# One hybrid diffusion trunk on one core: RG-LRU gate products in 64x64 quarters of TensorE, the scan result rounded on VectorE, the first norm kept off GpSimd, modulation weights loaded in halves

## The chip, the cores and the metric

The kernel runs on one core of one Trainium2 chip. The time is device microseconds of one execution. Five engines run side by side, each in the order of its own instruction list: TensorE (PE for its products, PEld for its weight loads), VectorE (DVE), ScalarE (ACT), GpSimd (POOL) and SyncE (SP), which here issues all transfers.

## The reference

Two layers of a trunk over 256 context and 256 latent tokens of width 1024. Each layer: a modulated RMS norm, an input projection, three token mixers (RG-LRU, gated linear attention, grouped attention), a gated merge, an output projection, then a modulated norm and an MLP. The change touches the modulation, the first norm and the RG-LRU:

```python
h = modulate(x, norm1_g, sh1, sc1)          # rms_norm(x, g) * (1 + scale) + shift
xh = xc.reshape(bn, n, LRU_BLOCKS, LRU_BLOCK_W)          # 16 blocks of 64 channels
r = sigmoid(einsum('bnhi,hij->bnhj', xh, a_w) + a_b)
i = sigmoid(einsum('bnhi,hij->bnhj', xh, x_w) + x_b)
log_a = -RGLRU_C * r * softplus(-lam)
u = sqrt(-expm1(2.0 * log_a)) * (i * xc)
# h_t = exp(log_a_t) * h_(t-1) + u_t, forward and backward; y = (h_0 + h_1) * gelu(y_in)
```

The inputs are float32. The gates exist for two directions, so each 128-channel tile of `xc` has four products with block-diagonal weights: two 64x64 blocks each.

## The kernel before

Activations are held with channels on the 128 partitions, in 8 tiles of width 1024/8, and with all 512 tokens along the row (in the last layer mixers whose context output nobody reads use the last 256 tokens only, `c0 = 256`). A float32 product of width 1024 is made of float32r products: operands are split into a rounded part and a rest (`hh`/`hl`, `wh`/`wl`), and `gemm` (L256) issues three matmuls of 512 columns for each of 8 channel tiles. A weight tile is loaded by SP (`weight_raw`, L189, three buffers), rounded by ACT (L200) and its rest taken by DVE (L201), into three pairs of buffers.

The order on each engine is fixed when the program is built: by a priority, which is the order of the Python code except where `tc.high_priority` moves weights ahead, and by when the builder thinks an operand is there. On the chip every engine runs its list in order and waits at each instruction for what it needs.

**Start.** `x` is loaded, `norm_stats` (L397) gives the inverse norm as a PSUM tile `st[0]` and as an SBUF copy `st[1]`. Four loads of 2 MB, `mq[0]` to `mq[3]` (`mod_load`, L381), bring modulation weights; `mod_half` multiplies each with the conditioning vector in 64 small matmuls of 32 array columns (L216, `mx<-modw,cs`: per channel tile four products, one for each quarter of the array's columns, each a pair of passes). Between the loads stand three weight loads for the first products. `norm_apply` (L429) runs in four calls of two channel tiles `k`: multiply by the inverse norm (odd `k` on GpSimd, L439, from the SBUF copy; even `k` on DVE, L441, from PSUM), scale and shift per half of the tokens (`k` in (0, 2, 5) on DVE, L446, the others on ACT, L448), then `split_to` (rounding on ACT, L307; rest on DVE, L308). `first_gemm` issues 18 matmuls after each call. The first call needs `mq[0]`, the second `mq[1]`, and so on.

**RG-LRU.** Channel tiles go in pairs. `lru_conv(i)` is one gemm, an ACT pass (L552) and three DVE passes (L555) which leave `xc`. `lru_gates(i)` (L558) loads the four 128x128 block-diagonal matrices and issues four float32 products of 128x512 (L566, two records each), each drained by an ACT tanh (L567); a further tanh (L571) and a DVE product (L572) follow per direction. Then come `lru_decay` (ACT Exp, L578), one Sqrt (L710), one or two `gate_y` gemms, and `lru_scan` for both tiles of the pair: L585, L586, scans L588 to L591, the sum L594, the gate L595 and `split_to` into `y1h`, `y1l`. The code's order is conv(i+1), gates(i), conv(i+2), gates(i+1), decay, sqrt, gate_y, scans; in the last pair the products `gla_kq(0)` take the place of the next conv, and the first head of the linear attention follows. The tanh tiles have room for two pairs, the gate products share four PSUM banks (`mx`).

Of the kernel before, what the change touches and what calls it, by code (L numbers as in the profile page):

```python
# [15 lines left out]
F32 = mybir.dt.float32  # L16
# [8 lines left out]
T = 512  # L25
# [16 lines left out]
NDVE = (0, 2, 5)  # L42
NL = 2
O_LX, O_LY, O_GQ, O_GK, O_GV, O_GR, O_GZ = 0, 1024, 2048, 2560, 3072, 4096, 5120
# [60 lines left out]
def trunk_kernel(ctx: ExitStack, tc: tile.TileContext, out: bass.AP, d: dict):  # L105
    nc = tc.nc
    V, S, G, P = nc.vector, nc.scalar, nc.gpsimd, nc.tensor
# [33 lines left out]
    def mx():  # L141
        return ps_mx.tile([128, 512], F32, name="mx")
# [46 lines left out]
    def weight_raw(*key):  # L189
        r = wraw.tile([128, 1024], F32, name="wraw")  # L190
        nc.sync.dma_start(r, d["wt"][order[key]])
        return r
# [110 lines left out]
                    mm(ps[t], hl[:, k, s], wh[:, i, :], start=False, stop=k == KT - 1)  # L303
        return ps

    def split_to(hi, lo, src):
        S.copy(hi, src)  # L307
        V.tensor_tensor(lo, src, hi.bitcast(F32), op=ALU.subtract)  # L308


# [67 lines left out]
        yield pace  # L378
        turn()

    def mod_load(l, u, h, tag):  # L381

        t = yp.tile([128, KT, 2, 256], F32, name="modw", tag=tag)
        nc.sync.dma_start(t, d["mod_w"][l, u, h].rearrange("p k (h c) -> p k h c", h=2))
        return t

    def mod_half(l, u, h, t):
# [38 lines left out]
        h = hp.tile([128, KT, 2, T], F32R, name="h")  # L426
        return (h[:, :, 0, :], h[:, :, 1, :], a, g, h)

    def norm_apply(l, which, x, c0, c1, st, hn, ks):  # L429
        n = c1 - c0  # L430
        sh0, sc0 = (0, 8) if which == 1 else (24, 32)
        hh, hl, a, g = hn[:4]
        k0, k1, s0, s1 = ks[0], ks[-1] + 1, c0 // 256, c1 // 256
        V.scalar_tensor_tensor(a[:, k0:k1, s0:s1], modT[l][:, sc0 + k0:sc0 + k1, s0:s1], 1.0, g[:, k0:k1, s0:s1],
                               op0=ALU.add, op1=ALU.mult)
        for k in ks:
            h = tmp()
            if k % 2:
                G.tensor_tensor(h[:, :n], x[:, k, c0:c1], st[1][:, :n], op=ALU.mult)  # L439
            else:  # L440
                V.tensor_tensor(h[:, :n], x[:, k, c0:c1], st[0][:, :n], op=ALU.mult)  # L441
            for s in range(s0, s1):
                c = slice(256 * s - c0, 256 * s - c0 + 256)
                sc, sh = a[:, k, s:s + 1], modT[l][:, sh0 + k, s:s + 1]
                if k in NDVE:
                    V.tensor_scalar(h[:, c], h[:, c], sc, sh, op0=ALU.mult, op1=ALU.add)  # L446
                else:
                    S.activation(h[:, c], h[:, c], AF.Identity, scale=sc, bias=sh)  # L448
            split_to(hh[:, k, c0:c1], hl[:, k, c0:c1], h[:, :n])

    hn1 = norm_mul(0, 1)
    mq = [mod_load(0, 0, 0, "yh")]
    raw = [weight_raw(0, "in", O_LY + 128 * i) for i in range(2)]
    mq.append(mod_load(0, 0, 1, "yl"))
    raw.append(weight_raw(0, "in", O_LY + 256))
    mq += [mod_load(0, 1, h, ("yh", "yl")[h]) for h in range(2)]
    first_ps = [ps_mm.tile([128, 512], F32, name="mm") for _ in range(3)]

# [8 lines left out]
    st = norm_stats(x1, 0, between=lambda: next(gs[0]))  # L469
    run(gs[0])  # L470
    next(gs[1])
    norm_apply(0, 1, x1, 0, T, st, hn1, range(2))
    run(gs[1])
    first = [weight_parts(r) for r in raw]
    for q in range(4):
        first_gemm(0, q)
        if q < 2:
            next(gs[q + 2])
        if q < 3:
            norm_apply(0, 1, x1, 0, T, st, hn1, range(2 * q + 2, 2 * q + 4))  # L480
        first_gemm(1, q)
        if q < 2:
            run(gs[q + 2])
        first_gemm(2, q)
# [30 lines left out]
    for l in range(NL):  # L515
# [27 lines left out]
            ge[i] = x[:, i, :256] if last else tmp()  # L543
            S.activation(ge[i], ps, AF.Gelu_apprx_tanh)

        xcs = {}

        def lru_conv(i):
            ps = gemm(weight(l, "in", O_LX + 128 * i, hi=E_LXH, lo=E_LXL, ahead=AHEAD if l or i > 1 else 0), hh, hl, 0)
# [4 lines left out]
            for k, (a, b) in ((0, (1, 256)), (2, (0, 255)), (3, (0, 254))):  # L554
                V.scalar_tensor_tensor(x3[:, :, a:b], p3[:, :, a + k - 1:b + k - 1], pc(l, "cw", 8 * k + i, 1),  # L555
                                       x3[:, :, a:b], op0=ALU.mult, op1=ALU.add)

        def lru_gates(i):  # L558
            xc = xcs.pop(i)
            gw = sm.tile([128, 4, 128], F32, name="gw")  # L560
            nc.sync.dma_start(gw, d["lruw"][l, i])
            rt, tt, ix = (t[:, i % 4] for t in ws_)
            for dd in range(2):
                for q, dst in ((0, rt), (1, ix)):
                    pg = mx()
                    P.matmul(pg, gw[:, 2 * dd + q, :], xc, start=True, stop=True)  # L566
                    S.activation(dst[:, dd, :], pg, AF.Tanh, scale=0.5,  # L567
                                 bias=habx[:, l, 16 * q + 8 * dd + i:16 * q + 8 * dd + i + 1])

                c2p = c2[:, l, 1, 8 * dd + i:8 * dd + i + 1]  # L570
                S.activation(tt[:, dd, :], rt[:, dd, :], AF.Tanh, scale=c2p, bias=c2p)  # L571
                V.scalar_tensor_tensor(ix[:, dd, :], ix[:, dd, :], 1.0, xc, op0=ALU.add, op1=ALU.mult)  # L572
# [7 lines left out]
        def lru_scan(i):  # L580
            rt, tt, ix = (t[:, i % 4] for t in ws_)
            for dd in range(2):
                a, u, h = rt[:, dd, :], tt[:, dd, :], ix[:, dd, :]

                V.scalar_tensor_tensor(u, a, 1.0, u, op0=ALU.add, op1=ALU.mult)  # L585
                V.tensor_tensor(u, u, h, op=ALU.mult)  # L586
                if dd == 0:
                    V.tensor_tensor_scan(h, a, u, 0.0, op0=ALU.mult, op1=ALU.add)  # L588
                else:
                    V.tensor_tensor_scan(h[:, 255::-1], a[:, 255::-1], u[:, 255::-1], 0.0, op0=ALU.mult, op1=ALU.add)  # L590
                    V.tensor_tensor_scan(h[:, 511:255:-1], a[:, 511:255:-1], u[:, 511:255:-1], h[:, 0:1],  # L591
                                         op0=ALU.mult, op1=ALU.add)
            y = rt[:, 0, c0:]
            V.tensor_tensor(y, ix[:, 0, c0:], ix[:, 1, c0:], op=ALU.add)  # L594
            V.tensor_tensor(y, y, ge[i], op=ALU.mult)  # L595
            split_to(y1h[:, i, c0:], y1l[:, i, c0:], y)


        wz = tmp1(F32, (128, KT, 32))
# [96 lines left out]
            gate_consts()  # L696
        for i in range(0, 8, 2):
            lru_conv(i + 1)
            if i < 6:
                lru_gates(i)  # L700
                lru_conv(i + 2)
            else:

                kq0 = gla_kq(0)
                lru_gates(i)
            lru_gates(i + 1)
            for j in range(2):
                lru_decay(i + j)
            tt = ws_[1][:, i % 4:i % 4 + 2]
            S.activation(tt, tt, AF.Sqrt, scale=0.25, bias=epsc)  # L710
            for j in range(LYS[l][i // 2 + 1]):
                gate_y(next(ly))
            if i == 6:
                gates0 = gla_gates(0)
                v0 = gla_v(0)
            for j in range(2):
                lru_scan(i + j)
            if i == 6:
                ys0 = gla_r(0)
            if i == GZP:  # L720
                zs = gla_z()
# [399 lines left out]
def layout(inp):  # L1121
# [52 lines left out]
        put(l, "qg", A["q_norm_g"][l])  # L1174
        put(l, "kg", A["k_norm_g"][l])
    a["par"] = par
    lruw = np.zeros((NL, 8, 128, 4, 128), f)
    for dd in range(2):
        for q, name in enumerate(("lru_a_w", "lru_x_w")):
            w = A[name][:, dd].reshape(NL, 8, 2, 64, 64)  # L1180
            for s in range(2):
                lruw[:, :, 64 * s:64 * s + 64, 2 * dd + q, 64 * s:64 * s + 64] = w[:, :, s]
    a["lruw"] = lruw
    glaw = np.zeros((NL, 3, 32, 2, 512), f)
    for dd in range(2):
# [36 lines left out]
```

## Time and profile before

| what | value |
|---|---|
| median of 3 runs | 1861.91 us (1858.67 to 1863.18) |
| profiled execution | 1860.73 us, its span 1858.9 us |
| mean granted TensorE clock | 0.993 |
| PE, PEld, DVE, ACT, POOL busy | 97%, 80%, 69%, 50%, 3% of the span |
| HBM read | 252.82 MB, 137 GB/s over the span |

Busy shares are averages over stages with different limits. PE records overlap (a matmul is followed by the next before its end), so a busy PE is read by the distance between starts rather than by durations. Between the profiled execution's own time and its span lie 1.8 us outside of the program's instructions.

### The profile page before, as it was taken

How to read it: one execution, taken by the hardware profiler on the slowest of the kernel's cores; microseconds unless marked ns; L12 is line 12 of the kernel's file. 1: busy time of each engine (PE TensorE's matmuls, PEld its weight loads, DVE VectorE, ACT ScalarE, POOL GpSimd, SP SyncE). 2: the span in 40 equal slices, each digit the busy share in tenths (PEclk: the TensorE clock that was granted, in tenths of full speed). 3: DMA queues.
4: the chain of work that ended last, by engine and by line, in shares of the span. 5: the costliest groups of instructions: out<-in, count | busy, mean ns of one | idle time of the engine just before them, and what ended most of it. 6: DMA issues, size and time to landing. Idle time of an engine off the chain costs nothing.

```text
span 1858.9 us, 26345 instructions
## 1 busy us (share of the span) xinstructions
PE 1803.0 (97%) x9992; PEld 1496.2 (80%) x9992; DVE 1288.0 (69%) x2206; ACT 936.3 (50%) x1620; POOL 62.8 (3%) x87
## 2 busy tenths in 40 slices
PE   5999999999999999999999999999999999999999
PEld 4766788888787888988888889767889877878887
DVE  4786775454557777789763447797876588778776
ACT  4787545333444333564332325788665455556443
POOL 1000000000000000000000000000000000000000
PEclk9999999999999999999999999999999999999999
DMA  8322222232211556666753235522333432755554
GB/s 324 102 76 85 70 82 80 70 102 80 68 57 52 196 188 201 215 219 208 237 178 100 91 95 184 173 92 85 109 101 122 131 125 91 261 170 159 186 188 148
DMA packets 82143, 255.59 MB, mean 137 GB/s; under 512 B 9184, under 2 KB 12384, under 8 KB 81248
## 3 DMA queue, kind: packets, MB, share of 16 engines
q1 hardware_dynamic: 82016, 253.90, 42.0%
q8 instruction: 79, 1.29, 0.3%
q14 instruction: 48, 0.39, 0.1%
HBM read 252.82 MB, written 1.05 MB: 137 GB/s over the span
## 4 chain that ended last, share of the span: by engine, by line
PE 59%; issue 22%; DVE 9%; ACT 7%; POOL 1%; DMA 1%; SPq 0%; POOLq 0%; DVEq 0%; ACTq 0%
PE mm L216 48%; PE mx L216 5%; DVE wl L201 2%; PE mx L841 2%; ACT lru L567 1%; PE mx L220 1%; PE mx L822 1%; ACT wh L200 1%; ACT lru L710 1%; DVE lru L586 1%; PE mx L566 1%; DVE lru L588 1%; ACT lru L571 1%; PE mx L793 1%; DMA wraw<-wt 1%
## 5 line engine op out<-in xcount | busy, mean ns | idle before, releaser
L216 PE MATMUL mm<-h,wh 128*128 128x512 f32 (+1 forms) x2512 | 729.6, 370 | 7.1 <-ACT h L307 5.1
L200 ACT CAST wh<-wraw 128x1024 fp32r<-128x1024 f32 x365 | 382.2, 1049 | 500.9 <-PE mm L216 391.5
L201 DVE TENSOR_TENSOR wl<-wraw,wh 128x1024 fp32r<-128x1024 f32 x365 | 445.5, 1222 | 235.6 <-ACT wh L200 219.9
L216 PEld LDWEIGHTS mm<-h,wh 128*128 128x128 f32 x2512 | 452.4, 189 | 91.5 <-issue 7.2
L216 PE MATMUL mm<-h,wl 128*128 128x512 f32 (+1 forms) x1448 | 493.9, 341 | 0.0
L216 PEld LDWEIGHTS mm<-h,wl 128*128 128x128 f32 x1448 | 274.0, 189 | 31.6 <-issue 1.4
L216 PE MATMUL mm<-yh,wh 128*128 128x512 f32 (+1 forms) x640 | 224.7, 351 | 2.2 <-DVE big L1039 2.1
L216 PE MATMUL mm<-yh,wl 128*128 128x512 f32 (+1 forms) x640 | 224.0, 350 | 0.0
L216 PE MATMUL mm<-yl,wh 128*128 128x512 f32 (+1 forms) x640 | 222.4, 348 | 0.0
L216 PE MATMUL mm<-yp,wh 128*128 128x512 f32 (+1 forms) x576 | 183.6, 374 | 2.5 <-ACT g L873 2.3
L216 PE MATMUL mm<-wh,h 128*128 128x512 f32 x576 | 183.4, 395 | 0.0
L216 PE MATMUL mm<-yp,wl 128*128 128x256 f32 x512 | 145.1, 283 | 0.0
L370 DVE SCALAR_TENSOR_TENSOR t<-t,cs,t 128x512 f32<-128x512 f32 x178 | 127.2, 746 | 25.6 <-DMA t<-mod_w 18.7
L216 PEld LDWEIGHTS mm<-yh,wh 128*128 128x128 f32 x640 | 121.7, 190 | 17.4 <-issue 3.0
L216 PEld LDWEIGHTS mm<-yh,wl 128*128 128x128 f32 x640 | 121.2, 189 | 15.4 <-issue 0.7
L216 PEld LDWEIGHTS mm<-yl,wh 128*128 128x128 f32 x640 | 121.2, 189 | 14.9 <-issue 0.5
L216 PEld LDWEIGHTS mm<-wh,h 128*128 128x128 f32 x576 | 107.7, 188 | 23.1 <-issue 1.0
L216 PEld LDWEIGHTS mm<-yp,wh 128*128 128x128 f32 x576 | 104.1, 189 | 24.0 <-ACT g L873 2.5
L216 PE MATMUL mm<-wl,h 128*128 128x512 f32 x288 | 113.4, 394 | 0.0
L216 PEld LDWEIGHTS mm<-yp,wl 128*128 128x128 f32 x512 | 96.9, 189 | 0.8 <-issue 0.7
L216 PE MATMUL mx<-t,t 128*128 128x128 f32 (+2 forms) x416 | 81.7, 338 | 0.1
L989 ACT ACTIVATE t<-mx,mxs,rsq 128x512 f32<-128x512 f32 (+1 forms) x48 | 33.9, 709 | 74.0 <-DVE mxs L987 72.0
(223 smaller groups left out, 2006.5 us busy)
## 6 DMA issues: line engine op xcount, KB each, us to landing
wraw<-wt SPq DMA_DIRECT2D x365, 512.0 KB, 3.6
t<-mod_w SPq DMA_DIRECT2D x144, 256.0 KB, 3.5
modw<-mod_w SPq DMA_DIRECT2D x6, 2048.0 KB, 14.4
big<-xt SPq DMA_DIRECT2D x8, 512.0 KB, 5.1
gw<-lruw SPq DMA_DIRECT2D x16, 256.0 KB, 3.7
out<-big SPq DMA_DIRECT2D x8, 128.0 KB, 1.9
t<-glaw SPq DMA_DIRECT2D x8, 96.0 KB, 2.9
t<-ropeg SPq DMA_DIRECT2D x2, 256.0 KB, 3.3
```

Of the source, the lines that this page charges most:

```text
L200: S.copy(wh, r)
L201: (G if lo == "G" else V).tensor_tensor(wl, r, wh.bitcast(F32), op=ALU.subtract)
L216: P.matmul(o, a, b, **kw)
L220: P.transpose(o, a, ident)
L370: V.scalar_tensor_tensor(a, t, c, a, op0=ALU.mult, op1=ALU.add)
L566: P.matmul(pg, gw[:, 2 * dd + q, :], xc, start=True, stop=True)
L567: S.activation(dst[:, dd, :], pg, AF.Tanh, scale=0.5, bias=habx[:, l, 16 * q + 8 * dd + i:16 * q + 8 * dd + i + 1])
L571: S.activation(tt[:, dd, :], rt[:, dd, :], AF.Tanh, scale=c2p, bias=c2p)
L586: V.tensor_tensor(u, u, h, op=ALU.mult)
L588: V.tensor_tensor_scan(h, a, u, 0.0, op0=ALU.mult, op1=ALU.add)
L841: P.matmul(po[:, :256], a, b, start=j == 0, stop=j == len(mm) - 1)
L989: S.activation(p[:, :128 * nk], psc[:, :128 * nk], AF.Exp, scale=r, bias=mxs[:, 1:2], accum_out=mxs[:, 2:3])
```

## The change

- Gate products: the weights of a channel tile shrink from four 128x128 block-diagonal matrices to two 128x128 stacks of 64x64 blocks (rows 0 to 63 the blocks of `a_w`, rows 64 to 127 those of `x_w`). Each direction has four 64x64 products, one in each quarter of the array, into two PSUM tiles. A quarter whose rows are not those on which its half of `xc` lies reads a copy with swapped halves, `xs`, which two new transfers per tile make after the conv; it takes a `gtmp` buffer.
- `split_to` takes the engine of the rounding; `lru_scan` passes VectorE.
- `n` is read before the gates of a pair; the loop that uses it stands where it stood.
- In the first norm odd tiles are multiplied on DVE from PSUM, and all scale-and-shift passes are on ACT.
- `mod_load` issues two transfers of 1 MB; the first weight load stands between the halves of `mq[1]`, the other two after it.

```diff
-    def split_to(hi, lo, src):
-        S.copy(hi, src)
+    def split_to(hi, lo, src, e="S"):
+        cp(e)(hi, src)
         V.tensor_tensor(lo, src, hi.bitcast(F32), op=ALU.subtract)
...
-    def mod_load(l, u, h, tag):
+    def mod_load(l, u, h, tag, between=lambda: None):
...
-        nc.sync.dma_start(t, d["mod_w"][l, u, h].rearrange("p k (h c) -> p k h c", h=2))
+        src = d["mod_w"][l, u, h].rearrange("p k (h c) -> p k h c", h=2)
+        nc.sync.dma_start(t[:, :4], src[:, :4])
+        between()
+        nc.sync.dma_start(t[:, 4:], src[:, 4:])
...
-            if k % 2:
+            if k % 2 and on_g:
                 G.tensor_tensor(h[:, :n], x[:, k, c0:c1], st[1][:, :n], op=ALU.mult)
...
-                if k in NDVE:
+                if k in NDVE and on_g:
                     V.tensor_scalar(h[:, c], h[:, c], sc, sh, op0=ALU.mult, op1=ALU.add)
...
-    mq = [mod_load(0, 0, 0, "yh")]
-    raw = [weight_raw(0, "in", O_LY + 128 * i) for i in range(2)]
-    mq.append(mod_load(0, 0, 1, "yl"))
-    raw.append(weight_raw(0, "in", O_LY + 256))
+    raw = []
+    mq = [mod_load(0, 0, 0, "yh"),
+          mod_load(0, 0, 1, "yl", lambda: raw.append(weight_raw(0, "in", O_LY)))]
+    raw += [weight_raw(0, "in", O_LY + 128 * i) for i in range(1, 3)]
...
+            xs = xss[i] = gtmp()
+            nc.sync.dma_start(xs[:64], xc[64:])
+            nc.sync.dma_start(xs[64:], xc[:64])
...
-            gw = sm.tile([128, 4, 128], F32, name="gw")
+            gw = sm.tile([128, 2, 128], F32, name="gw")
...
             for dd in range(2):
+                pgs = mx(), mx()
+                for q in range(2):
+                    r = slice(64 * q, 64 * q + 64)
+                    for b in range(2):
+                        P.matmul(pgs[q][64 * b:64 * b + 64, :], gw[r, dd, 64 * b:64 * b + 64],
+                                 (xc if b == q else xs)[r, :], start=True, stop=True)
                 for q, dst in ((0, rt), (1, ix)):
-                    pg = mx()
-                    P.matmul(pg, gw[:, 2 * dd + q, :], xc, start=True, stop=True)
+                    pg = pgs[q]
                     S.activation(dst[:, dd, :], pg, AF.Tanh, scale=0.5,
...
-            split_to(y1h[:, i, c0:], y1l[:, i, c0:], y)
+            split_to(y1h[:, i, c0:], y1l[:, i, c0:], y, "V")
```

## Rows read from the trace of the kernel before

**Rows 1.** The page: busy time, share of the span and instructions of each engine.
```profile
PE 1803.0 (97%) x9992; PEld 1496.2 (80%) x9992; DVE 1288.0 (69%) x2206; ACT 936.3 (50%) x1620; POOL 62.8 (3%) x87
```

**Rows 2.** PE timeline at a gate call: start, us, engine, line, tiles, count.
```profile
62.95 0.39 PE L216 MATMUL mm<-h,wl 128*128 128x512 f32 x1
63.18 3.60 PE L566 MATMUL mx<-t,gw 128*128 128x512 f32 x8
66.21 1.03 PE L216 MATMUL mm<-h,wh 128*128 128x512 f32 x2
67.07 0.39 PE L216 MATMUL mm<-h,wl 128*128 128x512 f32 x1
```

**Rows 3.** PE timeline at a group of small modulation products, then ACT behind it.
```profile
41.57 0.39 PE L216 MATMUL mm<-h,wl 128*128 128x512 f32 x1
41.89 1.96 PE L216 MATMUL mx<-modw,cs 128*32 128x128 f32 x64
43.77 0.73 PE L216 MATMUL mm<-h,wh 128*128 128x512 f32 x2
...
45.11 1.59 ACT L448 ACTIVATE t<-t,modT,amul 128x256 f32<-128x256 f32 x3 [0.94 <-DVE amul L434]
```

**Rows 4.** Busy time of each engine by stretch, both RG-LRU stages.
```profile
core 0: us, PE busy (x) PEld busy (x) DVE busy (x) ACT busy (x) POOL busy (x), PEclk, DMA share, GB/s
92.00:104.00 12.00, 12.00 (x42) 7.42 (x40) 11.47 (x17) 11.61 (x17) 0.00 (x0) 1.00 0.27 95
sum 151.00, PE 147.86 PEld 109.07 DVE 113.31 ACT 111.50 POOL 0.66; mean PE 18.48 PEld 13.63 DVE 14.16 ACT 13.94 POOL 0.08
...
1226.00:1255.00 29.00, 28.31 (x134) 20.18 (x133) 26.10 (x42) 24.30 (x34) 0.00 (x0) 1.00 0.30 92
sum 140.00, PE 131.87 PEld 99.36 DVE 115.92 ACT 115.09 POOL 0.93; mean PE 26.37 PEld 19.87 DVE 23.18 ACT 23.02 POOL 0.19
```

**Rows 5.** ACT and PE timelines at the last pair's gates, first layer.
```profile
159.38 0.59 ACT L667 ACTIVATE t<-mm 128x512 f32<-128x512 f32 x1
163.52 0.62 ACT L307 CAST yh<-lru 128x512 fp32r<-128x512 f32 x1 [3.55 <-DVE lru L595]
164.04 1.26 ACT L567 ACTIVATE lru<-mx,par 128x512 f32<-128x512 f32 x2
...
158.41 3.60 PE L566 MATMUL mx<-t,gw 128*128 128x512 f32 x8
164.78 5.40 PE L566 MATMUL mx<-t,gw 128*128 128x512 f32 x8 [2.77 <-ACT lru L567]
```

**Rows 6.** Waits of ACT in the first layer's stage, then in the second's.
```profile
ACT yh L307 <- DVE lru L595: 22.6, 8, 5.1
...
ACT yp L307 <- DVE lru L595: 8.7, 6, 3.1
```

**Rows 7.** Groups of instructions by line and shape: busy us, mean ns, idle before.
```profile
L567 ACT ACTIVATE lru<-mx,par 128x512 f32<-128x512 f32 x64 | 40.8, 684 | 1.1 <-PE mx L566 0.9
L571 ACT ACTIVATE lru<-lru,c 128x512 f32<-128x512 f32 x32 | 26.1, 817 | 0.0
L998 DVE COPY t<-mx 128x512 f32<-128x512 f32 x32 | 21.9, 684 | 4.3 <-PE mx L220 4.1
L769 DVE COPY t<-t 128x256 f32<-128x256 f32 x16 | 4.4, 286 | 0.0
L446 DVE TENSOR_SCALAR t<-t,amul,modT 128x256 f32<-128x256 f32 x21 | 11.9, 598 | 0.1
```

**Rows 8.** DVE timeline where the first gates get their input.
```profile
59.94 2.31 DVE L555 SCALAR_TENSOR_TENSOR t<-mm,par,t 128x510 f32<-128x510 f32 x3
```

**Rows 9.** DMA issues by line: engine, count, KB each, median us to landing.
```profile
wraw<-wt SPq DMA_DIRECT2D x365, 512.0 KB, 3.6
gw<-lruw SPq DMA_DIRECT2D x16, 256.0 KB, 3.7
out<-big SPq DMA_DIRECT2D x8, 128.0 KB, 1.9
t<-glaw SPq DMA_DIRECT2D x8, 96.0 KB, 2.9
```

**Rows 10.** Waits of the SP queue, first RG-LRU stage: us, times, longest.
```profile
SPq L191 <- DVE wl L201: 137.3, 22, 9.6
```

**Rows 11.** Timelines of the start: PE, then DVE, ACT and POOL.
```profile
21.23 0.40 PE L220 MATMUL mx<-ident,t 128*128 128x128 f32 x1
26.76 0.79 PE L216 MATMUL mm<-h,wh 128*128 128x512 f32 x1 [5.12 <-ACT h L307]
27.48 3.64 PE L216 MATMUL mx<-modw,cs 128*32 128x128 f32 x64
31.05 0.80 PE L216 MATMUL mm<-h,wh 128*128 128x512 f32 x1
...
23.94 2.11 DVE L446 TENSOR_SCALAR t<-t,amul,modT 128x256 f32<-128x256 f32 x2
...
18.07 1.05 ACT L200 CAST wh<-wraw 128x1024 fp32r<-128x1024 f32 x1 [0.21 <-DMA wraw<-wt]
23.52 1.09 ACT L448 ACTIVATE t<-t,modT,amul 128x256 f32<-128x256 f32 x2 [1.46 <-DVE amul L434]
24.65 0.62 ACT L307 CAST h<-t 128x512 fp32r<-128x512 f32 x1
...
22.14 5.04 POOL L439 TENSOR_TENSOR t<-big,t 128x512 f32<-128x512 f32 x4 [6.20 <-ACT t L419]
```

**Rows 12.** Busy time of each engine by stretch, two stretches of the start.
```profile
21.60:26.70 5.10, 0.04 (x1) 0.00 (x0) 4.83 (x9) 2.79 (x6) 4.56 (x4) 0.82 1.02 427
26.70:31.10 4.40, 4.34 (x66) 3.30 (x66) 3.37 (x4) 0.95 (x2) 0.48 (x1) 0.50 1.02 432
```

**Rows 13.** PE timeline where the first head of the linear attention begins, first layer.
```profile
207.24 0.39 PE L216 MATMUL mm<-h,wh 128*128 128x512 f32 x1
211.78 0.94 PE L793 MATMUL mx<-t,t 128*128 128x128 f32 x6 [4.14 <-DVE t L788]
```

More of the change, by code (lines that the diff above doesn't have):

```diff
@@ L427, in norm_mul, with norm_apply @@
         return (h[:, :, 0, :], h[:, :, 1, :], a, g, h)
-    def norm_apply(l, which, x, c0, c1, st, hn, ks):
+    def norm_apply(l, which, x, c0, c1, st, hn, ks, on_g=True):
         n = c1 - c0
@@ L471, in trunk_kernel @@
     next(gs[1])
-    norm_apply(0, 1, x1, 0, T, st, hn1, range(2))
+    norm_apply(0, 1, x1, 0, T, st, hn1, range(2), False)
     run(gs[1])
@@ L479, in trunk_kernel @@
         if q < 3:
-            norm_apply(0, 1, x1, 0, T, st, hn1, range(2 * q + 2, 2 * q + 4))
+            norm_apply(0, 1, x1, 0, T, st, hn1, range(2 * q + 2, 2 * q + 4), False)
         first_gemm(1, q)
@@ L544, in gate_y @@
             S.activation(ge[i], ps, AF.Gelu_apprx_tanh)
-        xcs = {}
+        xcs, xss = {}, {}
         def lru_conv(i):
@@ L556, in lru_conv @@
                                        x3[:, :, a:b], op0=ALU.mult, op1=ALU.add)
+            xs = xss[i] = gtmp()
+            nc.sync.dma_start(xs[:64], xc[64:])
+            nc.sync.dma_start(xs[64:], xc[:64])
         def lru_gates(i):
-            xc = xcs.pop(i)
-            gw = sm.tile([128, 4, 128], F32, name="gw")
+            xc, xs = xcs.pop(i), xss.pop(i)
+            gw = sm.tile([128, 2, 128], F32, name="gw")
             nc.sync.dma_start(gw, d["lruw"][l, i])
@@ L698, in trunk_kernel @@
             lru_conv(i + 1)
+            n = LYS[l][i // 2 + 1]
             if i < 6:
@@ L710, in trunk_kernel @@
             S.activation(tt, tt, AF.Sqrt, scale=0.25, bias=epsc)
-            for j in range(LYS[l][i // 2 + 1]):
+            for j in range(n):
                 gate_y(next(ly))
@@ L1176, in layout @@
     a["par"] = par
-    lruw = np.zeros((NL, 8, 128, 4, 128), f)
+    lruw = np.zeros((NL, 8, 128, 2, 128), f)
     for dd in range(2):
@@ L1181, in layout @@
             for s in range(2):
-                lruw[:, :, 64 * s:64 * s + 64, 2 * dd + q, 64 * s:64 * s + 64] = w[:, :, s]
+                lruw[:, :, 64 * q:64 * q + 64, dd, 64 * s:64 * s + 64] = w[:, :, s]
     a["lruw"] = lruw
```

## The prediction

> **What bounds the kernel now.** I read the page first: PE is busy for 97% of the span, DVE for 69%, ACT for 50% [rows 1]. So PE time that is removed counts, if DVE and ACT can follow in the stage where it is removed. Then the timelines of the stages that the change touches. In the first 50 us PE stands idle from 21.6 to 26.8 and after that does modulation products before it can go on with the first gemms [rows 11]. In the RG-LRU PE stands almost never, but the windows show that DVE is not far behind: 113.3 us busy in the 151 us of the first layer's stage, 115.9 in the 140 us of the second's, and 11.5 of 12 and 26.1 of 29 us in its densest parts [rows 4]. That is why I don't take PE's saving at its face.
>
> **Gate products.** One call takes from 63.18 to the start of the next gemm. That gemm's first two records start at 66.21 and about 66.84 (the third, at 67.07, less one step of 0.23), so its own work starts near 66.61 and the call takes 3.43 us: eight records, 0.43 us each [rows 2]. Sixteen calls are 54.9 us. After the change a direction has four products, eight records, one for each quarter. If the four quarters run at once a direction takes two passes, 0.86 us, and a call 1.71 us; if they take turns, a call has 16 passes, 6.86 us.
>
> Which of them holds? The trace has products in parts of the array, but of another cut: the modulation products of 32 columns and all 128 rows. Thirty-two products of 128 columns, 64 records, stand between gemm matmuls: from 41.80 (41.57 and a step of 0.23) to 43.77, 1.97 us [rows 3]. A 512-column pass takes 0.43, so one of 128 columns should take 0.107; 64 of them in turn would take 6.8 us, 16 groups of four at once 1.71. So quarters of the columns do run at once, each pair of passes beside the others, and what is left, 1.97 - 1.71 = 0.26 us, bounds the price of going into this mode and out again. Halves of the rows stand in no row of this trace. The bounds for a call are 1.71 + 0.26 = 1.97 us (all four at once) and 3.43 + 0.26 = 3.69 (columns at once, the halves of the rows in turn). I take 1.97: the two row halves read different partitions and write different PSUM tiles, as the column parts do that were seen to overlap. This saves PE 1.46 us a call, 11.7 us a layer, 23.4 in all.
>
> The Trainium skill speaks on both sides. "TensorEngine Tiling (Array Packing)", Tile-to-Partition Mapping, lists 64x64 as four independent tiles, which is the 1.97 us; no row here shows that cut. "TensorE: Matmul & The Clock Gate", Part 3, says that matmuls start and end strictly in program order. By that rule the second pass of one quarter would hold up the next quarter. The rows of the 32-column products contradict it so far: 32 pairs with each pair holding up the next would take at least 32 x 0.107 = 3.4 us, and 1.97 were measured.
>
> **What the quarters wait for.** Half of them read `xs`, which leaves SP only after the conv's last DVE pass. No transfer inside the chip stands in the trace; the nearest rows are 128 KB in 1.9 us, 96 KB in 2.9 and 256 KB in 3.7 [rows 9]. Two of 128 KB behind each other: 2 to 4 us; I take 3. For the first gates DVE ends `xc` at 59.94 + 2.31 = 62.25 and PE starts them at 63.18 [rows 2, 8], so `xs` comes some 2 us late. In the middle pairs the gates stand one gemm (5.4 us) behind their conv on PE, but PE will come 1.5 us earlier per call, so now and then PE will wait for `xs`. Behind a waiting SP instruction stand the weight loads; they already wait for DVE (22 times, 137 us, in the first stage [rows 10]) with three raw and three split tiles ahead, so a DVE wait among DVE waits costs nothing; without that cover it would cost the gemms the 3.6 us of a load. The `gw` load halves; reading `n` earlier does nothing.
>
> **Rounding on VectorE.** ACT loses 16 casts but, more than that, the wait in front of each: 22.6 us in the first stage, 8.7 in the second, all for DVE's L595 [rows 6]. While it waits, the gate tanh stands behind it on ACT. Once that reaches PE: at 159.97 ACT was free for the tanh, but it stood before the cast until 163.52; the gates of the last tile began at 164.78 and took 5.40 instead of 3.60 [rows 5]. Without the wait they would have begun at 158.41 + 3.43 = 161.84 and ended at 165.3; they ended near 170.0, so 4.7 us were lost. ACT needs some 3.8 us for a call (four times 0.6 and twice 0.7, the durations of [rows 7] less their overlap), more than PE's new 1.97. Where two calls stand back to back, as here, the second finds its first two banks free 2.2 us after the first call's start and the other two at 4.1, and ends at 4.9 instead of 3.9: 1.0 us stays, 3.7 are to be gained. DVE gets a copy: by the strided SBUF row 0.29 for 256, 0.57 for 512; by the PSUM row 0.68 [rows 7]. I take 0.57 and 0.29: 4.6 us of DVE in the first layer, 2.3 in the second.
>
> **How much DVE lets through.** First layer: PE's stage could shrink by 11.7 + 3.7 = 15.4 to 136; DVE then has 113.3 + 4.6 = 118 us of work, 87% where it was 75%. Second layer: 140 - 11.7 = 128; DVE 118, 92% where it was 83%. Each conv product waits for DVE's L555, which stand between scans. At 87% I let three quarters through, 12 us (the late `xs` included); at 92% a third, 4 us. Bounds: nothing, and all of it. Where PE gets ahead, the next late thing is DVE's chain into the first head: there PE waits 4.1 us already [rows 13].
>
> **Start.** GpSimd's four products take 22.14 to 27.18, and beside them two DVE passes that elsewhere take 0.6 each take 2.11 together [rows 7, 11]. Without GpSimd tile 0 goes over ACT: two passes (1.09) from 23.52, a cast of 0.62, so its first matmul starts near 25.3 instead of 26.76. The larger part is the second modulation group: 27.48 to 31.05, at a granted clock of 0.50, that is 1.2 GHz, after PE had stood idle for 5.1 us in which the clock fell [rows 11, 12]. With 427 GB/s [rows 12], and the second of the early weights landed by 18.07 [rows 11], `mq[1]` (2.1 MB) lands near 22.9. After the change 0.5 MB less stands ahead of its end: 21.7. Its products then fit into the idle stretch, half of them earlier still. PE had 71 gemm matmuls, two groups and little else after 31.05: 16.1 + 4.0 + 0.3, to 51.4. Now it can begin near 25.3, but ACT sets the pace: per tile 1.09 + 0.62, over eight tiles 13 us, and two weight casts; and `mq[3]` lands no earlier, near 34.0 (the last early weight at 22.9 + 0.5 MB, 24.1, and two tiles of 2.1 MB behind it, 9.8). The last two tiles are ready after the group (2.0), the way from it to ACT (43.77 to 45.11, 1.3 [rows 3]), ACT (3.3) and DVE's rest (0.6): 41.2; 18 matmuls (4.1 us) then end at 45.3 at the earliest; with two stalls of about a microsecond 47.3. That is 4 us, between nothing (ACT's 13 us fully exposed) and 6. In the last layer the half loads save nothing: their products are not what PE waits for.
>
> **Sum.** -4 (start) -12 -4 = -20 from the profiled 1860.7: 1841. The median of the runs lies 1.2 above that execution: 1842.
>
> **Rivals** (times with the same 1.2 us added). (a) Everything goes through: 4 + 15.4 + 11.7 + the other stalls of the second stage, some 4: 35 us, 1827. For it: ACT no longer waits for DVE, and scans may lag by a pair. Against it: DVE at 92%. (b) The halves of the rows take turns, or pairs hold each other up: a call takes 3.69, 16 x 0.26 = 4 us more; the start and the ACT wait stay gained (4 + 3.7): 1858. By the rule of strict order ("TensorE: Matmul & The Clock Gate", Part 3) this would be the case; rows 3 speak against it for columns. (c) `xs` comes late every time, slower than before: PE holds its order, and each of 16 calls waits. The gain outside of it is 4 + 3.7 + 23.4 = 31 us, so it decides from 1.9 us of exposed wait per call; at 3 us, a whole transfer, 48 - 31 = +17: 1879. For it: DVE's L555 end just ahead of the gates [rows 8]. Against it: between conv and gates stands a gemm of 5.4 us in 12 of 16 calls, and the order is made with the transfer in it. (d) The quarters don't overlap: 16 x (6.86 + 0.26 - 3.43) = +59 less 7.7: 1913; rows 3 speak against it.
>
> **Chances and range.** Forecast 0.62, (a) 0.14, (b) 0.12, (c) 0.09, (d) 0.03. The forecast's own range is 1833 to 1851. The range over cases is 1824 to 1859; it leaves out (c) and (d). A difference under 0.3%, 5.6 us, can't be told from no change here: faster is the forecast, (a) and a third of (b), 0.80; same the rest of (b), 0.08; slower 0.12.
>
> **What would show it.** Right: eight gate records of a direction within about 1.1 us, in groups of four that start together; gate calls of 2 us between gemms; no cast of `lru` on ACT and no ACT wait for L595; the first gemm near 25 us and the first conv gemm about 4 us earlier; DVE's share of both stages near 90%. Wrong: records of a direction spread over 1.7 us or 3.4; PE waits for `xs`; the heads of the linear attention begin no earlier because DVE's scans end when they did; a longer wait than 4.1 us there.

## The result, and the profile after

The changed kernel takes 1871.99 us (median of 5 runs, 1868.85 to 1873.53) where the kernel before takes 1862.34 on the same chip: ratio 1.0055 with an interval of 1.0042 to 1.0068. It is slower by half a per cent, more than can be told from no change; 1842 was predicted. Its profiled execution has a span of 1868.7 us against 1858.9.

The page's busy times (the row that answers to [rows 1]) say little: TensorE is as busy as before, although its gate products got shorter.

```profile
PE 1804.9 (97%) x10120; PEld 1484.4 (79%) x10120; DVE 1289.2 (69%) x2220; ACT 935.3 (50%) x1612; POOL 65.6 (4%) x83
```

Three numbers that every profile gives, span, PE's busy time and mean granted clock, can be turned into an account that adds up. Idle is span less busy. What the clock took is (1 - mean clock) x span, since the lower level is half of the upper one. Work is busy less that: what PE would need at full clock. (The clock has three digits, so that column is good to about 0.9 us; half-clock time in which PE stands idle is in it too.)

| kernel | span | PE busy | idle | clock took | work |
|---|---|---|---|---|---|
| before | 1858.9 | 1803.0 | 55.9 | 13.0 (0.993) | 1790.0 |
| changed | 1868.7 | 1804.9 | 63.8 | 20.6 (0.989) | 1784.3 |

Work fell by some 6 us, not by 23; idle rose by 8, and the clock took 8 more. These three differences are the result. The times of some events show where (start of the instruction named, us, from the traces):

| event | before | changed |
|---|---|---|
| first conv's first DVE pass, layer 0 | 59.9 | 59.1 |
| last scan of the RG-LRU, layer 0 | 202.3 | 203.1 |
| first conv's first DVE pass, layer 1 | 1184.8 | 1187.8 |
| last scan of the RG-LRU, layer 1 | 1311.6 | 1323.7 |
| last gemm matmul | 1854.8 | 1864.4 |

**A call that goes as costed.** PE's timeline of the changed kernel (start, us, engine, line, tiles, shape, count) at one call in layer 0, the counterpart of [rows 2]:

```profile
72.04 0.39 PE L216 MATMUL mm<-h,wl 128*128 128x512 f32 x1
72.36 0.64 PE L578 MATMUL mx<-t,gw 64*64 64x512 f32 x1
72.37 0.65 PE L578 MATMUL mx<-g,gw 64*64 64x512 f32 x2
72.38 1.05 PE L578 MATMUL mx<-t,gw 64*64 64x512 f32 x2
...
73.72 0.59 PE L578 MATMUL mx<-t,gw 64*64 64x512 f32 x1
74.24 0.73 PE L216 MATMUL mm<-h,wh 128*128 128x512 f32 x2
```

The previous gemm's last matmul needs 0.23 us, so the call takes from 72.27 to 74.24, 1.97 us for 16 passes: four quarters at once, starts 0.43 to 0.48 us apart. Counted to where the next gemm's own work starts, as the 3.43 us of the prediction were, it is 2.08 (its third record starts at 74.81, less two steps of 0.23). Seven of the 16 calls go through undivided like this.

**A call that does not.** The same view later in the layer, and then SP and DVE over the same microseconds. The bracket is PE's idle time and what ended it (the first one is put down to a cast; DVE's row shows that `xc` was what came last).

```profile
98.00 0.39 PE L216 MATMUL mm<-h,wl 128*128 128x512 f32 x1
100.46 1.04 PE L578 MATMUL mx<-t,gw 64*64 64x512 f32 x2 [2.07 <-ACT wh L200]
102.66 1.80 PE L578 MATMUL mx<-g,gw 64*64 64x512 f32 x3 [1.16 <-DMA g<-t]
...
106.75 0.73 PE L216 MATMUL mm<-h,wh 128*128 128x512 f32 x2
```

```profile
100.43 0.47 SPq L563 DMA_DIRECT2D g<-t  x1
100.95 0.59 SPq L564 DMA_DIRECT2D g<-t  x1
```

```profile
98.38 0.72 DVE L558 SCALAR_TENSOR_TENSOR t<-mm,par,t 128x510 f32<-128x510 f32 x1
99.02 0.68 DVE L609 TENSOR_TENSOR lru<-lru 128x512 f32<-128x512 f32 x1
99.62 0.73 DVE L558 SCALAR_TENSOR_TENSOR t<-mm,par,t 128x508 f32<-128x508 f32 x1
```

Before the change the same call came later than its input (PE, then DVE):

```profile
100.78 3.60 PE L566 MATMUL mx<-t,gw 128*128 128x512 f32 x8
98.88 0.74 DVE L555 SCALAR_TENSOR_TENSOR t<-mm,par,t 128x508 f32<-128x508 f32 x1
```

`xc` was ready at 99.62, 1.2 us ahead of PE; at the call of 133.18 it was 0.6 us. At these two calls that was all the slack there was.

In the changed kernel PE is at the call at 98.23. The conv's passes alternate on DVE with a scan tile's sum and end at 100.35; SP issues the copies then, and PE, which holds its order, waits again until 102.66. The windows (length, then busy time and count by engine, and the granted clock behind POOL's column) show what follows:

```profile
core 0: us, PE busy (x) PEld busy (x) DVE busy (x) ACT busy (x) POOL busy (x), PEclk, DMA share, GB/s
98.20:103.00 4.80, 1.57 (x4) 0.38 (x4) 4.80 (x9) 2.35 (x4) 0.00 (x0) 1.00 0.57 176
103.00:106.40 3.40, 3.40 (x14) 1.03 (x12) 2.19 (x4) 1.70 (x3) 0.00 (x0) 0.51 0.27 59
```

TensorE stood for most of 4.4 us, and for the next 3.4 its granted clock is 0.51, that is 1.2 GHz: the passes come 0.85 us apart (two of them at 104.29 and 105.14). The call lasts 8.5 us (98.23 to 106.75) where [rows 2] has 3.43. "TensorE: Matmul & The Clock Gate" of the Trainium skill, Part 1, says that an idle TensorE falls to half rate; this trace agrees, with the 0.51.

The waits of PE in layer 0's stage (line, releaser, us in total, times, longest):

```profile
PE mx L578 <- DMA g<-t: 3.5, 3, 1.2
PE mx L578 <- ACT wh L200: 2.1, 1, 2.1
PE mx L578 <- ACT lru L582: 0.8, 1, 0.8
```

And the largest at the gates in layer 1's stage and first head, which grew far more:

```profile
PE mx L578 <- ACT lru L582: 2.6, 2, 1.8
PE mx L578 <- DVE t L558: 1.8, 1, 1.8
PE mx L578 <- DMA g<-t: 0.6, 1, 0.6
```

The releaser in the bracket is not always the one that held PE. In the two layers some 5 us of these waits end 0.1 to 0.3 us behind their conv's last DVE pass, that is, they are for `xc`; 4.1 us are for the copy and 2.6 us for PSUM banks that ScalarE's tanh drains (at 165.84 `xc` and a bank come at the same time). Besides, seven calls are cut: their first product, or first two, run alone (1.0 us each), with gemm matmuls or a wait before the others.

In this stage the clock stands at half from 103.0, 137.2 and 167.9, 3.4 us each; before there was one such stretch, from 164.8. In layer 1's stage and first head the stretches rise from one (1318.6) to three (1222.6, 1287.5 for 6.8 us, 1331.8).

**The transfer** itself is what was assumed (DMA issues: count, KB each, us to landing):

```profile
g<-t SPq DMA_DIRECT2D x32, 128.0 KB, 2.3
```

**Start.** PE's timeline, the counterpart of [rows 11]:

```profile
19.02 1.08 PE L216 MATMUL mx<-modw,cs 128*32 128x128 f32 x32
23.94 0.74 PE L216 MATMUL mm<-h,wh 128*128 128x512 f32 x2 [3.84 <-ACT wh L200]
24.61 1.94 PE L216 MATMUL mx<-modw,cs 128*32 128x128 f32 x32
...
46.69 1.22 PE L216 MATMUL mm<-h,wh 128*128 128x512 f32 x4 [0.82 <-ACT h L307]
```

The first gemm starts at 23.94, earlier than forecast, and half of the second modulation group is in the idle stretch; but its other half still runs at half clock (1.94 us for what takes 1.08 at 19.02), and PE waits for ScalarE's casts at the end. The first conv's DVE pass begins 0.8 us earlier, not 4, and even that says little: it begins at 58.7 to 60.6 in the eleven kernels with this start and at 58.2 to 59.9 in the five with the old one.

### The profile page after: what moved, and what is told of

The parts are those of the page before. It is cut to its first block, busy times and chain, and to the rows that moved or that the text cites. A ratio compares the mean times of both kernels' runs of the same rounds, so it can differ in the third digit from the quotient of the medians.

```text
span 1868.7 us, 26690 instructions
## 1 busy us (share of the span) xinstructions
PE 1804.9 (97%) x10120; PEld 1484.4 (79%) x10120; DVE 1289.2 (69%) x2220; ACT 935.3 (50%) x1612; POOL 65.6 (4%) x83
## 5 line engine op out<-in xcount | busy, mean ns | idle before, releaser
L216 PEld LDWEIGHTS mm<-yp,wh 128*128 128x128 f32 x576 | 105.2, 191 | 24.4 <-ACT g L889 2.9
```

The lines of the kernel that those rows point to most:

```text
L216: P.matmul(o, a, b, **kw)
```

## The experiments

Every ratio is to the kernel before on the same chip. The first four set "theory W" (TensorE waits for the swapped copy) against "theory D" (VectorE and ScalarE hold the stages, so PE's saving is not passed on). Later ones call the first "theory P", since the traces had shown the clock behind the pauses. The account at the end of this section has all of them.

**Without the quarters** (the start's part and the rounding stay):

```diff
-                        P.matmul(pgs[q][64 * b:64 * b + 64, :], gw[r, dd, 64 * b:64 * b + 64],
-                                 (xc if b == q else xs)[r, :], start=True, stop=True)
...
+                    P.matmul(pg, gw[:, 2 * dd + q, :], xc, start=True, stop=True)
```

> The changed kernel with the gate products as before (four full 128x128 products per tile, no swapped copy); rounding on VectorE, the first norm without GpSimd and the half loads stay. Theory W (the quarters lose because the swapped copy arrives late, PE stands before it, and the granted clock falls to one half behind these stands): the loss goes away and what the other parts gain is left, 1850 to 1858 us, and the granted clock stays at 1.0 in both RG-LRU stages. Theory D (VectorE is what holds both stages, and the rounding on it makes them longer): 1865 to 1872, little changed from the changed kernel.

Measured: 1863.94 us, ratio 1.0008 [0.9991, 1.0026]. Between the theories, and the other parts give nothing in sum. The trace has a gain and a loss: the last scan of layer 0 begins at 194.1 instead of 202.3, that of layer 1 at 1314.0 instead of 1311.6, though its layer was entered 2.7 us earlier.

**The quarters alone** (before, with the new gate products and `xs`):

> The kernel before with the gate products in quarters and the swapped copy by two transfers, and nothing else of the change. Theory W: the quarters carry the whole loss and more, 1870 to 1880. Theory D: PE time is saved and VectorE has no more work than before, 1845 to 1860.

Measured: 1876.09 us, ratio 1.0078 [1.0058, 1.0098]. The loss belongs to the quarters with their copy.

**Quarters without the copy.** All quarters read `xc`; half of the gate products are so over the wrong 64 channels.

```diff
-            xs = xss[i] = gtmp()
-            nc.sync.dma_start(xs[:64], xc[64:])
-            nc.sync.dma_start(xs[64:], xc[:64])
...
-                                 (xc if b == q else xs)[r, :], start=True, stop=True)
+                                 xc[r, :], start=True, stop=True)
```

> The changed kernel without the swapped copy: all four quarters read the conv result itself, so half of the gate products are taken over the wrong 64 channels, and there is no transfer and no wait for it. Theory W: the quarters give what they were costed at less what VectorE holds back, 1838 to 1852, gate calls of about 2 us. Theory D: 1862 to 1872, since VectorE's work is the same.

Measured: 1857.69 us, ratio 0.9978 [0.9965, 0.9991]. In between again: 14 us better than the changed kernel, so the copy cost that much; but some 17 short of what the shorter products should give against the kernel without the quarters. The account: work 1769.3, 20.7 less than before, so the 23.4 us of the prediction are nearly all there. Idle is 67.1 (+11) and the clock took 22.3 (+9). PE's waits in layer 0's stage:

```profile
PE mx L574 <- ACT lru L582: 3.5, 1, 3.5
PE mx L574 <- ACT t L555: 2.5, 1, 2.5
```

Even without a copy PE comes to its gates before the conv's passes are through. All five waits at the gates in the two layers (15.5 us) end 0.1 to 0.3 us behind the conv's last pass on DVE, whatever the bracket names. The longest of them, in layer 1 (PE, then DVE):

```profile
1277.76 1.98 PE L574 MATMUL mx<-t,gw 64*64 64x512 f32 x8 [3.99 <-ACT lru L589]
1276.93 0.72 DVE L558 SCALAR_TENSOR_TENSOR t<-mm,par,t 128x508 f32<-128x508 f32 x1
```

**The copy by VectorE**, two copies of 64x512 instead of the transfers:

```diff
-            nc.sync.dma_start(xs[:64], xc[64:])
-            nc.sync.dma_start(xs[64:], xc[:64])
+            V.tensor_copy(xs[:64], xc[64:])
+            V.tensor_copy(xs[64:], xc[:64])
```

> The changed kernel with the swapped copy made by two VectorE copies of 64x512 instead of two transfers. Theory W: the copy costs VectorE some 0.7 us a tile but comes 2 us earlier, 1848 to 1860. Theory D: VectorE has 11 us more work in all, 1872 to 1885.

Measured: 1869.56 us, ratio 1.005 [1.0034, 1.0067]. VectorE's busy time rises by 13.5 us for 32 copies, 0.42 each; a shorter copy on an engine that is itself late gains 2.4 us, within the spread of the runs. This one tells the theories apart badly.

**The start alone** (halves of the modulation loads, first norm without GpSimd):

> The kernel before with the start's part alone: modulation weights in halves, the first norm without GpSimd. Two theories now. Theory P (pauses): the time is TensorE's work plus its pauses plus what the clock takes after a pause; the traces so far put 1 us of gain at the start and some 4 us into the last layer's modulation, where the half clock lasted 3.4 us instead of 6.8 in every kernel with half loads. By it 1856 to 1859 against 1862. Theory N (nothing): the start gives less than 1 us and the rest of the trace's differences are the builder's order; 1860 to 1863.

Measured: 1860.09 us, ratio 0.9998 [0.9984, 1.0011]: nothing. In its trace the first conv's pass even begins 0.6 us later than before.

**The rounding, layer by layer**, on the kernel before:

```diff
+            split_to(y1h[:, i, c0:], y1l[:, i, c0:], y, "S" if last else "V")
```

> The kernel before with the scan result rounded by VectorE in the first layer only. Theory P: ScalarE no longer stands for the rounding while gate tanhs wait behind it; the kernel without quarters gained 5 to 6 us in this layer's RG-LRU by it: 1855 to 1858. Theory D (VectorE holds the stage): one more copy per tile, 0.4 us each, takes back what ScalarE gives: 1860 to 1865.

Measured: 1857.7 us, ratio 0.9984 [0.9971, 0.9997]. Three microseconds gained, and the wait of 2.8 us of PE for ScalarE's tanh at the last pair [rows 5] is gone from the list. The stage shortens by 7.0 us (142.4 to 135.4); more than half of that is lost again behind it.

> The kernel before with the scan result rounded by VectorE in the last layer only. The kernel without quarters lost 5 us in this layer's RG-LRU and 7 us in the first head behind it, with 13.6 us more at half clock. Theory P: the copies make VectorE's chain late, TensorE pauses in three places and at the first head, and its clock falls: 1868 to 1874. Rival: that loss was the order that the builder chose for the start's part, not the rounding: 1859 to 1864.

Measured: 1867.26 us, ratio 1.0033 [1.0017, 1.005]. The last layer loses some 6 us, twice what the first gains. PE's waits in its stage and first head:

```profile
PE mx L793 <- DVE t L788: 5.8, 2, 2.9
PE mx L566 <- issue: 2.0, 1, 2.0
PE mx L566 <- ACT t L552: 1.8, 1, 1.8
PE mx L566 <- DVE t L555: 1.7, 1, 1.7
```

Before, the first of these is 3.5 us, once.

**No copy, and every product over its own channels.** The off-diagonal quarters leave the second gate with its 64-channel halves swapped in PSUM, and ScalarE's tanh reads them from there in two instructions:

```diff
+                for s in range(2):
+                    r, o = (slice(64 * p, 64 * p + 64) for p in (s, s ^ 1))
+                    S.activation(ix[r, dd, :], pgs[1][o, :], AF.Tanh, scale=0.5, bias=hb[1][r])
```

> The changed kernel without the swapped copy, and with the right result: the off-diagonal quarters leave the second gate with its halves swapped in PSUM, and ScalarE's tanh reads it in two halves of 64 partitions, each written to the other half. Two more ScalarE instructions per call, some 1.2 us. If the transfer alone was the trouble, the time is that of the kernel without the swapped copy, 1854 to 1863. If ScalarE's tanh now holds the PSUM banks (its work per call 5 us where the quarters take 1.9), 1863 to 1872.

Measured: 1877.96 us, ratio 1.0088 [1.0069, 1.0107], slower than either expectation. Work is the second lowest of all (1766.1), idle the highest (82.0). PE at the last pair's calls, layer 0:

```profile
160.38 1.95 PE L574 MATMUL mx<-t,gw 64*64 64x512 f32 x16
169.67 3.69 PE L574 MATMUL mx<-t,gw 64*64 64x512 f32 x16 [7.34 <-issue]
```

The first call takes 1.95 us, then PE stands 7.3 us, and the second runs at half clock. No releaser is shown. These are the last tanh of the first call on ACT and the second call's last conv pass on DVE:

```profile
165.23 1.38 ACT L580 ACTIVATE lru<-mx,par 64x512 f32<-64x512 f32 x2
168.85 0.72 DVE L558 SCALAR_TENSOR_TENSOR t<-mm,par,t 128x508 f32<-128x508 f32 x1
```

The banks were free at 166.6, but `xc` was ready only at 169.57, and PE started 0.1 us later. So it was not ScalarE's drain, as the second expectation has it, that held the call to the end, but again the conv's passes between the scans; the pauses of 6.3 us (at 102.5) and 4.0 us (at 1294.7) end in the same way.

**Gates one conv later.** Both convs of a pair and the first of the next now stand before a pair's gates:

```diff
+        lru_conv(1)
         for i in range(0, 8, 2):
-            lru_conv(i + 1)
...
             if i < 6:
+                lru_conv(i + 2)
                 lru_gates(i)
-                lru_conv(i + 2)
+                lru_conv(i + 3)
```

> The changed kernel with every gate call one conv later: both convs of a pair and the next pair's first conv stand before its gates, so that the swapped copy has a gemm more to come in. Theory P (TensorE's saving is lost in pauses and in the clock behind them, because gates stand too close to the conv): the calls become 1.9 us each, fewer falls of the clock, 1845 to 1858. Theory D (VectorE and ScalarE hold the RG-LRU whatever the order): 1862 to 1874.

Measured: 1843.76 us (1842.98 to 1847.29), ratio 0.9916 [0.9901, 0.9931]: 26 us better than the changed kernel by the ratios, 28 by the medians (the two were not run side by side), and better than the kernel before and than theory P's range. All waits of PE in layer 0's stage:

```profile
PE mx L810 <- DVE t L805: 4.3, 1, 4.3
PE mx L655 <- ACT lru L582: 0.2, 1, 0.2
PE mx L578 <- ACT lru L582: 0.2, 1, 0.2
```

The gates wait 0.2 us in all, and 3.6 us in layer 1, each time for a bank that ScalarE drains; no call of either layer waits for its conv or its copy any more, and none is cut after its first product. From the first conv's DVE pass (60.3) to the last scan (189.8) layer 0 takes 129.5 us instead of 142.4, layer 1 (1174.8 to 1296.3) 121.5 instead of 126.9. VectorE is busy for 126.7 of the 151 us of layer 0's stage where it was 113.3 [rows 4]: it could do more than it was given, which is what theory D denied.

> The kernel without the swapped copy (half of the gate products are over the wrong 64 channels) with the same later gates. Theory P: the full saving of TensorE, some 21 us, less what VectorE still lets through: 1838 to 1850. Theory D: no better than the same kernel with the gates in the old place, 1855 to 1860.

Measured, without the copy (half of the gate products over the wrong 64 channels): 1840.94 us, ratio 0.9895 [0.9881, 0.9909]. With the later gates the copy costs 3 us instead of 14.

> The kernel before with the later gates, as a control of the order alone. Theory P: before has pauses of 2.8 us or more in two places of the RG-LRU only, so little is to be had: 1857 to 1862. Theory D: moving work between the engines' lists only shifts the waits, 1860 to 1866.

Measured, the order alone on the kernel before: 1861.85 us, ratio 1.0003 [0.9993, 1.0013]. The order by itself gives nothing; the quarters need it.

**What is left in the last layer.** With the later gates one pause stands out there, between the last pair's two calls (PE's timeline of that kernel):

```profile
1256.14 0.59 PE L578 MATMUL mx<-t,gw 64*64 64x512 f32 x1
1259.82 1.11 PE L578 MATMUL mx<-t,gw 64*64 64x512 f32 x1 [3.09 <-ACT lru L582]
```

The clock then stands at half for 10.2 us, from 1258.8. Three versions of it: rounding on VectorE in the first layer only; the first head's V products between the two calls; both.

```diff
                 kq0 = gla_kq(0)
                 lru_gates(i)
+                v0 = gla_v(0)
             lru_gates(i + 1)
```

> The changed kernel with the later gates, rounding on VectorE in the first layer only. With the gates in their old place the last layer's rounding cost 6.7 us. If VectorE's extra copies make the first head's operands late wherever the gates stand: 1836 to 1841. If the later gates have taken that wait away: 1842 to 1847.

> The changed kernel with the later gates, and the first head's V products between the last pair's two gate calls. In the last layer TensorE paused 3.7 us between them for a PSUM bank that ScalarE had to drain, and ran 10.2 us at half clock. Theory P (the pause and the clock behind it are what is left to gain): 3.7 us of pause and up to 5.1 of clock, 1836 to 1841. Rival (VectorE and ScalarE are as far behind, and the pause comes back at the first head): 1842 to 1848.

> Both: rounding on VectorE in the first layer only, V products between the last pair's gate calls. If the two losses of the last layer are apart from each other, 1831 to 1838. If they are the same wait seen twice, no better than the better of the two, 1836 to 1842.

Measured: 1853.39 us, ratio 0.9951 [0.9937, 0.9965]; 1865.21, 1.0014 [1.0005, 1.0024]; 1873.45, 1.0057 [1.0043, 1.0071]. All three are worse than the version that they start from, outside of every expectation. The first has a wait that was in neither kernel; here PE, last layer:

```profile
1239.11 1.11 PE L578 MATMUL mx<-g,gw 64*64 64x512 f32 x1 [4.85 <-DVE t L635]
```

Within a gate call PE waits for the `mx` bank of `gla_z`, which DVE's L635 reads. ScalarE shows what else came back; here its cast, ahead of the same call's tanh, and then all its waits of that kind in the last layer's stage and first head:

```profile
1237.91 0.40 ACT L307 CAST yp<-lru 128x256 fp32r<-128x256 f32 x1 [4.58 <-DVE lru L610]
ACT yp L307 <- DVE lru L610: 13.8, 7, 4.6
```

That is the wait which the rounding on VectorE takes away ([rows 6] had 8.7 us in this layer, the version that this one starts from has none), and the layer's stage is 8.1 us longer. The second has no pause between the calls any more, but a longer one behind them. Here PE in the last layer, then the instruction on DVE that it waits for:

```profile
1317.00 0.79 PE L216 MATMUL mm<-h,wh 128*128 128x256 f32 x2 [11.98 <-DVE g L701]
```

```profile
1316.54 0.40 DVE L701 SCALAR_TENSOR_TENSOR g<-g,mm 128x256 f32<-128x256 f32 x1
```

L701 is 0.40 us long and drains a bank of the gemms; it stood on VectorE behind some 15 us of scans and head work. Why these are late shows on PE at the last pair's two calls, layer 0:

```profile
151.18 0.64 PE L578 MATMUL mx<-t,gw 64*64 64x512 f32 x1
175.04 0.64 PE L578 MATMUL mx<-t,gw 64*64 64x512 f32 x1
```

The V products fill 21.9 us between the calls, where a pause of 3.1 us was to be filled. The last tile's gates come that much later and its scans with them: the last scan begins at 207.3 instead of 189.8.

The account of all profiles, made as in the first section:

| kernel | median | idle | clock took | work |
|---|---|---|---|---|
| without the quarters | 1863.94 | 57.0 | 18.6 | 1786.5 |
| quarters alone | 1876.09 | 69.1 | 24.4 | 1782.0 |
| no copy | 1857.69 | 67.1 | 22.3 | 1769.3 |
| copy by VectorE | 1869.56 | 62.2 | 24.3 | 1781.3 |
| start alone | 1860.09 | 55.9 | 16.8 | 1788.6 |
| rounding, first layer | 1857.70 | 53.4 | 13.0 | 1790.1 |
| rounding, last layer | 1867.26 | 62.5 | 14.9 | 1788.9 |
| shift by ScalarE | 1877.96 | 82.0 | 28.1 | 1766.1 |
| gates later | 1843.76 | 53.3 | 16.6 | 1771.8 |
| no copy, gates later | 1840.94 | 53.3 | 12.9 | 1772.4 |
| order alone | 1861.85 | 57.7 | 14.9 | 1786.1 |
| gates later, first rounding | 1853.39 | 61.5 | 14.8 | 1774.5 |
| gates later, V between | 1865.21 | 72.7 | 22.4 | 1770.0 |
| both | 1873.45 | 77.4 | 33.7 | 1761.8 |

Every kernel without the copy or with later gates has 15 to 28 us less work than before (the order alone, without quarters, apart); whether it is faster is decided by the two columns in the middle. (In the last row the clock's share holds much idle time, so its work is too low.)

The length of the two RG-LRU stages, from the first conv's first DVE pass to the start of the last scan:

| kernel | layer 0 | layer 1 |
|---|---|---|
| before | 142.4 | 126.9 |
| changed | 144.1 | 135.9 |
| without the quarters | 135.4 | 131.9 |
| quarters alone | 145.7 | 136.9 |
| no copy | 134.1 | 132.5 |
| gates later | 129.5 | 121.5 |
| no copy, gates later | 129.5 | 121.9 |

In the old place the quarters gain next to nothing in these stages even without their copy (third row against fifth); one conv later they shorten both, with the copy.

## Why the prediction was wrong

- **Gate products: right.** A call that finds its operands takes 1.97 us as forecast, and the work without the copy fell by 20.7 of 23.4 us. (The 1.97 end at the next gemm's first record and the 3.43 at its own work; counted alike, 2.08 and 1.35 us a call, 21.6 in all.) Rivals (b) and (d) are out. By the rule of strict order in "TensorE: Matmul & The Clock Gate", Part 3, of the Trainium skill, the second pass of a quarter would hold up the next; the trace does not agree: the first passes of four quarters start within 0.02 us at 72.36. (Both passes of a quarter come from one `P.matmul`, and in a cut call they run next to each other between gemm matmuls, so they are taken to be neighbours in PE's list; the trace shows starts and not the list.)
- **What the quarters wait for: this step failed.** The duration was right (3 us taken, 2.3 from issue to landing, and two issues 0.5 apart), the exposure was not. "Now and then PE will wait" had no term of its own in the sum (it was put into the three quarters let through), on the ground that a gemm of 5.4 us stands between conv and gates. That cover is not free time: ScalarE's pass and DVE's three passes come first, the latter between scans, and in the call shown above `xc` ended 2.1 us after PE had come for it; the copy begins only then. Before, the same call had 1.2 us of slack; PE reached the gates earlier by the 1.46 us that it saves per call, so the saving alone ate the slack, and the copy came on top. Nine of 16 calls were cut or stalled, two of them for PSUM banks alone; seven lost part of their fourfold rate (lone products take 1.0 us), and the clock fell behind the pauses, which no term of the sum held. The copy is only a part of it: without it the gates still waited 15.5 us for `xc`. Rival (c), at 0.09, had the sign and part of the mechanism; its price (a whole transfer in every call, 1879) was too high for the transfer and left out the clock.
- **How much DVE lets through: right in size, for another order.** 12 and 4 us were allowed; with the later gates the two stages shorten by 12.9 and 5.4, which is near by luck, since the order is another. In the changed kernel the stages grew by 1.7 and 9.1: there the limit was the place of the gates, not how much VectorE can do.
- **Rounding: right in the first layer, wrong in the last.** 3.7 us were to be gained at the last pair, less DVE's copies; 3 were measured (a copy takes 0.42 us of DVE where 0.57 were taken). The last layer was taken to be neutral and cost 6 to 7. Yet with the later gates taking it out there cost 6 to 10 us (ratio 0.9951 against 0.9916, 1853.4 against 1843.8, not run side by side), and ScalarE stood 13.8 us before its casts. So it has no price of its own. The lists of waits suggest what decides (the gates' tanhs behind a cast on ScalarE, or the conv's passes behind a copy on VectorE); no run separates it from the rest of the lists.
- **Start: mis-sized.** 4 us forecast, none in the time of the start alone, and in the traces no more than their spread. The first gemm came earlier than forecast, but the half group at half clock and ScalarE's casts stand behind it; where the rest of the 4 us went stays open.
- **Sum.** -20 was forecast and +10 measured. The 26 to 28 us between the changed kernel and that with later gates, whose code differs in nothing but the order of the calls, are nearly the whole error of 30; that order alone, without quarters, is worth nothing. With it the waits for `xc` and the copy are gone. That the quarters come too close to their operands is therefore shown. How much of a pause's cost is the pause and how much the clock behind it was read from the account alone; the one run that filled a pause put seven times its length into it. An edit also makes the builder list the rest anew, and how much of each difference is that list stays open.

## What to carry to other kernels

A saving on an engine that runs its list in order brings it sooner to the next thing that it must wait for: before counting it, take the slack between producer and consumer at that place, subtract the saving and each new step of the chain (here a transfer of 2.3 us), and if little is left, move the consumer later as part of the change. Read every version by the three numbers work, idle and clock, which tell a change that saves nothing from one whose saving is lost again. A bracket names one releaser, so look up the end of every operand before you believe it. The price of a small edit in one version does not hold in another, so judge combinations by their own run.

## What the runs showed of the hardware

- Pauses in a stage that is otherwise dense were followed by half clock for 3.4 us, in some places for 6.8 or 10.2 us. In the changed kernel two pauses of 0.4 and 1.2 us with one lone product between them (135.0 to 137.2) were followed by 3.4 us. A window of the version with later gates, behind its pause of 3.1 us, in which the clock had fallen at 1258.8:

```profile
1264.00:1269.10 5.10, 5.10 (x14) 3.38 (x11) 5.10 (x10) 5.07 (x8) 0.00 (x0) 0.50 0.14 57
```

PE is busy in all of this window, and the granted clock is still 0.50. In the kernel before, a pause of 2.6 us that ended at 1279.4 was followed by no fall.
- Products of 64x64 run four at once in all four quarters, rows and columns, with float32 in two passes: 16 passes in 1.97 us; the two passes of one quarter that stand alone between gemm matmuls cost 1.0 us.
- A transfer of 128 KB that moves 64 partitions to the other half lands 2.3 us after its issue (median of 32); VectorE copies the same in 0.42 us.
